# S5's state blocks worked two at a time in a one-core RWKV-7 / S5 / mixture-of-experts kernel

## The chip, the cores and the metric

The kernel runs on one core of one Trainium2 chip. The metric is the device time of one execution in microseconds (us), taken as the median of several runs. The engines are named as in the profile: PE is TensorE (PEld its weight loads), DVE is VectorE, ACT is ScalarE, POOL is GpSimd, SP issues the large DMAs.

## The reference

The layer works on 256 positions of width 2048. One input projection feeds two branches, whose results are merged by gates; a mixture of 32 experts follows. The part that is changed is the S5 branch, a linear recurrence of complex states that is diagonal and so runs state by state:

```python
a_bar = jnp.exp(lam * step)
b_bar = ((a_bar - 1.0) / lam)[..., None] * lax.complex(b_re, b_im)
bu = lax.complex(einsum('btgh,gph->btgp', uf, real(b_bar)), einsum('btgh,gph->btgp', uf, imag(b_bar)))
_, xs = lax.associative_scan(combine, (a_elems, bu), axis=1)      # x[t] = a_bar * x[t-1] + bu[t]
y = (einsum('btgp,ghp->btgh', real(xs), c_re) - einsum('btgp,ghp->btgh', imag(xs), c_im) + d_skip * uf)
z = jax.nn.gelu(y)
return (z @ w_glu_v) * jax.nn.sigmoid(z @ w_glu_g)
```

There are 64 groups of 16 channels, each with 64 states. The other branch is RWKV-7 time mixing with 16 heads; `y_a` of it, the S5 result and the gates give `mixed`, `x + mixed @ w_out` goes into the experts, and a last RMS norm ends the layer.

## The kernel before

**Stages.** The program has a front (projection, both branches, merge, `w_out`) and the experts behind it. In the front, the stream `front()` multiplies the normalised input with 66 blocks of 128 columns of `w_in` and one of 32 (`mm<-hT` in the trace: 48 products of 128x256 per block, 16 times three in float32r, from a high and a low half of weights and input). Its order is written out in `ORDER`: the S5 inputs u0 to u7 spread among r, k, v of the first eight heads, then eight blocks of gate b, then r, k, v of the last eight heads, the other eight blocks of gate b (gb8 to gb15), the sixteen of gate a, then the GLU of S5 (`glu`, which needs S5's result z) and RWKV's output product (`ro`, which needs both halves of RWKV).

**S5.** `s5()` prepares constants and then runs three generators over 32 blocks of 128 states (q = 0 to 31; four blocks belong to one 128-channel block of u, kb). `tabs` makes for each q a table E of sines and cosines on ACT and DVE. `prod` issues `bu_of(q)`: two float32 products with 32 rows of u as contraction and 128 columns of states, into one PSUM tile of three (`ps5`). `vec` turns them with the table (two products of 128x512 from PSUM), adds, runs two scans over the 256 positions, and turns back. `prod` then issues `out_of(q)`: four float32 products, 128 states onto 32 output channels, accumulated into rows 32(q mod 4) of a PSUM tile `yp` that four blocks share, after which `skip_of` adds the skip term on DVE. In the trace a float32 product shows as two MATMUL records. `s<-u,ring` is `bu_of`, `s<-vring,CR` is `out_of`.

**Order of the work.** Nothing is reordered at run time: a planner in Python emits all the instructions of the front. Every call passes `Paced.__getattr__`, which gives the operation a cost; `Timeline` keeps a planned clock for each engine; and the loop over `streams` (lines 1177 to 1199) picks, for each engine, the waiting operation with the earliest planned start less a bonus of its stream. The bonus of S5's streams is 0, or `B_P` = 0.4 when S5 is behind a straight line from `Z0` to `Z1` on DVE's planned clock. The RWKV stream has 0.5 and the weight splitting 0.5; on PE every stream but `front()` has 0.2.

**Slots.** Large tiles come out of one pool of `NA` = 18 slots of 128x2048 (`slot`, `free`, `room`). A stream that finds no free slot yields until one comes free. `places` asks for a slot when `front()` comes to blocks 0 and 8 of a gate; `rwkv(hf)` asks for one for each of its stages (AB, ts, ug, R for its first and second chunk c), and gives R back at the end of a chunk, BK after c=1's last scores, and four more at its end. S5 holds CR, ring and vring to its end (`free(3)` at p = 31). Slots of gate b come free when gb7 and gb15 have been stored to HBM. In every turn of the planner's loop the streams are asked in the order front, weight splits, evacuations, S5, RWKV.

Of the kernel before, what the change touches and what calls it, by code (L numbers as in the profile page):

```python
# [128 lines left out]
class Paced:  # L129
# [5 lines left out]
    def __getattr__(self, name):  # L135
        f = getattr(self._e, name)

        def g(*a, **k):
# [9 lines left out]
            if self._k == "pe":  # L148
                if name == "transpose":
                    c = 0.85e-3 * n  # L150
                else:
                    r, w = k["rhs"], k["lhsT"]
                    c = 0.42e-3 * n if r.dtype == F32R else 1.68e-3 * max(n, 64)
                    if w.shape[1] <= 64:
                        c *= 0.5 if w.shape[1] == 64 else 0.3
# [4 lines left out]
            elif name == "dma_start":  # L160
                c = 1.0
            else:
                fast = name in ("tensor_scalar", "tensor_copy", "memset")
                c = 0.07 + n * (0.52e-3 if fast else 6.3e-3 if name == "reciprocal" else 1.04e-3)
                own = 0.1
# [49 lines left out]
def hybrid_block(ctx: ExitStack, tc: tile.TileContext, x, win, win32, par, lora, gup, sb, sc, wglu, wro, wout,  # L215
# [323 lines left out]
    def s5():  # L539
# [78 lines left out]
        def tables(q):  # L618

            E = ring[:, q % 3 * 512:q % 3 * 512 + 512].rearrange("p (a t) -> p a t", a=2)  # L620
            act.activation(E[:, 0], iot, AF.Copy, scale=c["fh"][:, q:q + 1])
            act.activation(E[:, 1], iot, AF.Identity, scale=c["f"][:, q:q + 1], bias=c_magic)
            dve.scalar_tensor_tensor(E[:, 0], E[:, 1], MAGIC, E[:, 0], op0=OP.subtract, op1=OP.subtract)
            dve.scalar_tensor_tensor(E[:, 0], iot, c["fl"][:, q:q + 1], E[:, 0], op0=OP.mult, op1=OP.subtract)
            act.activation(E[:, 1], E[:, 0], AF.Identity, bias=c_magic)
            dve.scalar_tensor_tensor(E[:, 0], E[:, 1], MAGIC, E[:, 0], op0=OP.subtract, op1=OP.subtract)
            act.activation(E[:, 1], E[:, 0], AF.Sin, scale=-TWO_PI)
            act.activation(E[:, 0], E[:, 0], AF.Abs)
            act.activation(E[:, 0], E[:, 0], AF.Sin, bias=c_hpi, scale=-TWO_PI)
            return E  # L630
# [4 lines left out]
        def bu_of(q):  # L635
            kb, qi = divmod(q, 4)
            bu = ps5()
            if qi == 0 and kb < 7:
                load_b(kb + 1)
            for a in range(2):  # L640
                pe.matmul(bu[:, a * T:(a + 1) * T], lhsT=Bt[kb][32 * qi:32 * qi + 32, a],
                          rhs=u_of(kb)[32 * qi:32 * qi + 32], start=True, stop=True)
            return bu

        def out_of(q, pA, pB, yp):
            qi = q % 4
            for i, (cv, r) in enumerate(((CRv, pA[:, :T]), (CRv, pB[:, T:]), (CINv, pB[:, :T]), (CINv, pA[:, T:]))):
                pe.matmul(yp[32 * qi:32 * qi + 32, :T], lhsT=cv[:, q], rhs=r, start=(i == 0), stop=(i == 3))
# [12 lines left out]
        def tabs():  # L661
            for q in range(32):
                while q > at["prod"] + 2:
                    yield "wait"
                Es[q] = tables(q)
# [3 lines left out]
        def vec():  # L669
            for q in range(32):  # L670
                while at["tab"] <= q or at["bu"] <= q or q > at["out"] + 1:
                    yield "wait"
                E, bu = Es.pop(q), bus.pop(q)
                wv = vring[:, q % 2 * 1024:q % 2 * 1024 + 1024]
                V1, V2 = wv[:, 0:2 * T], wv[:, 2 * T:]
                b3 = bu.rearrange("p (a t) -> p a t", a=2)
                dve.tensor_mul(V1.rearrange("p (a t) -> p a t", a=2), b3, E[:, 0:1].to_broadcast([128, 2, T]))
                dve.tensor_mul(V2.rearrange("p (a t) -> p a t", a=2), b3, E[:, 1:2].to_broadcast([128, 2, T]))
                step("mul")
                dve.tensor_add(V1[:, :T], V1[:, :T], V2[:, T:])  # L680
                dve.tensor_sub(V1[:, T:], V1[:, T:], V2[:, :T])
                rho = c["rho"][:, q:q + 1].to_broadcast([128, T])
                dve.tensor_tensor_scan(V2[:, :T], rho, V1[:, :T], 0.0, op0=OP.mult, op1=OP.add)
                dve.tensor_tensor_scan(V2[:, T:], rho, V1[:, T:], 0.0, op0=OP.mult, op1=OP.add)
                z3 = V2.rearrange("p (a t) -> p a t", a=2)
                dve.tensor_mul(V1.rearrange("p (a t) -> p a t", a=2), z3, E[:, 0:1].to_broadcast([128, 2, T]))
                dve.tensor_mul(V2[:, :T], V2[:, :T], E[:, 1])
                dve.scalar_tensor_tensor(V2[:, T:], V2[:, T:], -1.0, E[:, 1], op0=OP.mult, op1=OP.mult)
                prods[q] = (V1, V2)
# [3 lines left out]
        def prod():  # L693
            for q in range(34):
                if q < 32:
                    while "u%d" % (q // 4) not in done or q > at["mul"] + 1:
                        yield "wait"
                    bus[q] = bu_of(q)
                    step("bu")
                    yield  # L700
                p = q - 2
                if p >= 0:
                    while at["prod"] <= p:
                        yield "wait"
                    if p % 4 == 0:
                        yps[p // 4] = ps5()
# [1001 lines left out]
```

## Time and profile before

| | us |
|---|---|
| median of 3 runs | 1851.1 (1850.18 to 1858.23) |
| the profiled execution | 1850.9 |
| its span, first to last instruction | 1849.1 |
| PE busy | 1521.7 (82%) |
| DVE busy | 831.8 (45%) |
| ACT busy | 570.5 (31%) |
| granted TensorE clock, mean | 0.885 |

The span falls in two parts: the front up to about 862 us and the experts behind it. Read the two apart: the averages of the table mix a part that PE fills with one that the DMA engines fill. A row of a timeline gives the start, the length, the engine, the line (166 for all, as every call passes one helper), the operation, the tile written, the tiles read, partitions and columns, and how many instructions are merged in the row. PE's spans overlap, since products are pipelined; the distance from one start to the next is what a product costs the engine.

### The profile page before, as it was taken

To read this page: it belongs to the slowest core of one execution; us is meant where nothing else is said; L and a number is where in the kernel's file an instruction comes from. 1 tells how busy PE (TensorE), PEld (TensorE's weight loads), DVE (VectorE), ACT (ScalarE), POOL (GpSimd) and SP (SyncE) were. 2 spreads that over 40 slices of the span, in tenths; PEclk is the share of its full clock that TensorE was granted. 3 is DMA by queue.
4 is the path that set the end of the run, shared out by engine and by line. 5 is a ranking of instruction groups with operands and counts; after the bars stand their busy time and mean duration, and the time that the engine had idled before them with its cause. 6 is when DMAs were issued, how large, how long until landed. Compare 5 with 4: busy or idle time off the path is not lost.

```text
span 1849.1 us, 29765 instructions
## 1 busy us (share of the span) xinstructions
PE 1521.7 (82%) x12604; PEld 995.9 (54%) x12604; DVE 831.8 (45%) x1349; ACT 570.5 (31%) x937; POOL 33.6 (2%) x64
## 2 busy tenths in 40 slices
PE   7999999999999999998867776666676677676673
PEld 6987998777999989986523222222222232211120
DVE  6887998777875457645022121222212121212123
ACT  6557664556744344443201100001000010000002
POOL 0000001000001000000000000000000000000000
PEclk9999999999999999998888877779877787778766
DMA  6543464232456347855899999999999999999993
GB/s 230 166 149 103 141 204 127 69 98 92 160 163 197 106 129 284 296 166 194 332 421 420 420 421 421 421 420 420 421 420 421 421 420 421 420 421 420 421 420 159
DMA packets 94955, 534.11 MB, mean 289 GB/s; under 512 B 10528, under 2 KB 10544, under 8 KB 45024
## 3 DMA queue, kind: packets, MB, share of 16 engines
q1 hardware_dynamic: 91792, 522.49, 72.2%
q0 software_dynamic: 3024, 9.64, 1.8%
q8 instruction: 102, 1.67, 0.4%
q14 instruction: 37, 0.30, 0.0%
HBM read 526.82 MB, written 5.28 MB: 288 GB/s over the span
## 4 chain that ended last, share of the span: by engine, by line
PE 48%; DMA 47%; DVE 2%; ACT 1%; issue 1%; SPq 0%; POOL 0%; DVEq 0%; ACTq 0%
PE mm L166 26%; DMA wt<-in_mgu_dram 23%; DMA wt<-in_md_dram 12%; PE s L166 11%; DMA wx<-in_mgu_dram 7%; PE sd L166 6%; DMA wx<-in_md_dram 4%; PE gu L166 2%; PE tr L166 1%; PE y L166 1%; DVE wl L166 1%; PE sc L166 1%; DMA x<-in_x_dram 1%; DMA ts<-ad 0%; DVE acc L166 0%
## 5 line engine op out<-in xcount | busy, mean ns | idle before, releaser
L166 PE MATMUL mm<-hT,wh 128*128 128x256 f32 x2144 | 395.7, 286 | 1.8 <-DVE hT L166 1.8
L166 PEld LDWEIGHTS mm<-hT,wh 128*128 128x128 f32 x2144 | 329.0, 188 | 23.3 <-issue 16.3
L166 DVE TENSOR_TENSOR wl<-wr,wh 128x1024 fp32r<-128x1024 f32 x213 | 259.9, 1220 | 164.5 <-ACT wh L166 162.0
L166 PE MATMUL gu<-wt,xg 128*32 128x256 f32 x2896 | 239.6, 462 | 102.6 <-DMA wt<-in_mgu_dram 93.0
L166 ACT CAST wh<-wr 128x1024 fp32r<-128x1024 f32 x213 | 222.4, 1044 | 270.2 <-PE mm L166 185.9
L166 PE MATMUL mm<-hT,wl 128*128 128x256 f32 x1072 | 301.7, 281 | 1.4 <-DVE wl L166 1.4
L166 PEld LDWEIGHTS gu<-wt,xg 128*32 128x32 f32 x2896 | 89.5, 126 | 225.2 <-DMA wt<-in_mgu_dram 141.9
L166 PEld LDWEIGHTS mm<-hT,wl 128*128 128x128 f32 x1072 | 201.8, 188 | 2.0 <-DVE wl L166 2.0
L166 DVE TENSOR_TENSOR acc<-acc,sc 128x1024 f32<-128x1024 f32 x128 | 150.5, 1218 | 94.6 <-PE sc L166 94.6
L166 DVE SCALAR_TENSOR_TENSOR hd<-gu,gs,hd 64x256 f32<-64x256 f32 x32 | 15.7, 491 | 319.1 <-ACT hd L166 268.9
L166 DVE SCALAR_TENSOR_TENSOR ys<-y,gs,ys 128x512 fp32r<-128x512 f32 x32 | 24.0, 751 | 273.7 <-ACT ys L166 273.7
L166 PE MATMUL gu<-wx,xg 128*32 128x256 f32 x1200 | 103.8, 479 | 44.5 <-DMA wx<-in_mgu_dram 43.1
L166 ACT ACTIVATE ys<-y,gs 128x512 fp32r<-128x512 f32 x32 | 22.0, 687 | 280.1 <-PE y L166 280.1
L166 ACT ACTIVATE hd<-gu,gs 64x256 f32<-64x256 f32 x32 | 15.0, 468 | 259.1 <-PE gu L166 258.8
L166 PEld LDWEIGHTS gu<-wx,xg 128*32 128x32 f32 x1200 | 37.9, 129 | 97.9 <-DMA wx<-in_mgu_dram 67.5
L166 PE MATMUL sc<-ys,ogT 32*128 32x512 f32 x512 | 56.0, 513 | 27.2 <-DVE acc L166 25.7
L166 ACT ACTIVATE xg<-tr,prm 128x256 f32<-128x256 f32 x64 | 26.9, 471 | 159.1 <-PE tr L166 143.0
L166 PE MATMUL s<-vring,CR 128*32 128x256 f32 x256 | 61.6, 382 | 0.8 <-DVE vring L166 0.8
L166 ACT CAST ogT<-tr 128x256 fp32r<-128x256 f32 x32 | 11.8, 373 | 162.9 <-PE tr L166 162.8
L166 PEld LDWEIGHTS sc<-ys,ogT 32*128 32x128 f32 x512 | 23.8, 215 | 61.8 <-issue 40.4
L166 ACT ACT_TABLE_LOAD x38 | 48.8, 1283 | 1.4 <-PEq L1696 0.7
L166 PEld LDWEIGHTS tr<-oh,xn 128*128 128x128 f32 x256 | 35.3, 205 | 15.3 <-issue 14.1
(460 smaller groups left out, 2159.1 us busy)
## 6 DMA issues: line engine op xcount, KB each, us to landing
wt<-in_mgu_dram SPq DMA_DIRECT2D x181, 1024.0 KB, 19.8
wt<-in_md_dram SPq DMA_DIRECT2D x87, 1024.0 KB, 19.8
wx<-in_mgu_dram SPq DMA_DIRECT2D x75, 1024.0 KB, 19.8
wr<-in_win_dram SPq DMA_DIRECT2D x132, 512.0 KB, 3.7
wx<-in_md_dram SPq DMA_DIRECT2D x41, 1024.0 KB, 19.8
wr<-in_wglu_dram SPq DMA_DIRECT2D x32, 512.0 KB, 3.9
wr<-in_wout_dram SPq DMA_DIRECT2D x32, 512.0 KB, 3.9
wr<-in_wro_dram SPq DMA_DIRECT2D x16, 512.0 KB, 6.9
```

The costliest lines, as they stand in the source:

```text
L166: return self._tl.do(Op(self._k, lambda: f(*a, **k), c, outs, ins, own, fn, name == "dma_start"))
```

## The change

S5 runs over 16 pairs of state blocks (p = 0 to 15) instead of 32 blocks. `bu_of(p)` issues its four products alternating between two groups of 32 rows, into two PSUM tiles; `out_of(p)` issues its eight alternating between two groups of 32 output columns. On ACT and DVE, the steps that need no per-block scalar run on both blocks in one instruction; those that do, the products from PSUM and the scans, stay one per block. The tables take 1024 columns of ring per pair; vring becomes two slots (so S5 holds four slots); the columns of b get a buffer of their own. `prod` runs one pair ahead instead of two blocks. In the planner, `w_in`-type products cost 0.465 ns a column instead of 0.42, float32 products 1.82 instead of 1.68 with a factor 0.5 where either side of the weights is 64 or less (before: 0.5 for 64 output columns, 0.3 for fewer), scans 2.1 instead of 1.04, and `Z1` is 470 instead of 400.

```diff
-                    c = 0.42e-3 * n if r.dtype == F32R else 1.68e-3 * max(n, 64)
-                    if w.shape[1] <= 64:
-                        c *= 0.5 if w.shape[1] == 64 else 0.3
+                    c = 0.465e-3 * n if r.dtype == F32R else 1.82e-3 * max(n, 64)
+                    if r.dtype != F32R and min(w.shape[0], w.shape[1]) <= 64:
+                        c *= 0.5
...
-        ring, vring = slot("ring"), slot("vring")
+        ring, vr = slot("ring"), [slot("vring") for _ in range(2)]
...
-            Bt[kb] = ring[:, 1536 + kb % 2 * 256:1792 + kb % 2 * 256].rearrange("p (a m) -> p a m", a=2)
+            Bt[kb] = stile([128, 2, 128], "Bt")
...
+            E = ring[:, p % 2 * 1024:p % 2 * 1024 + 1024].rearrange("p (q a t) -> p q a t", q=2, a=2)
+            for x_ in range(2):
+                q = 2 * p + x_
+                act.activation(E[:, x_, 0], iot, AF.Copy, scale=c["fh"][:, q:q + 1])
+                act.activation(E[:, x_, 1], iot, AF.Identity, scale=c["f"][:, q:q + 1], bias=c_magic)
+            E0, E1 = E[:, :, 0], E[:, :, 1]
+            dve.scalar_tensor_tensor(E0, E1, MAGIC, E0, op0=OP.subtract, op1=OP.subtract)
...
+            kb, half_ = divmod(p, 2)
+            bu = [ps5(), ps5()]
...
+                for x_ in range(2):
+                    pr = slice(64 * half_ + 32 * x_, 64 * half_ + 32 * x_ + 32)
+                    pe.matmul(bu[x_][:, a * T:(a + 1) * T], lhsT=Bt[kb][pr, a], rhs=u_of(kb)[pr], start=True, stop=True)
...
+            for i, (cv, v, a) in enumerate(((CRv, V1, 0), (CRv, V2, 1), (CINv, V2, 0), (CINv, V1, 1))):
+                for x_ in range(2):
+                    q = 2 * p + x_
+                    pe.matmul(yp[32 * (q % 4):32 * (q % 4) + 32, :T], lhsT=cv[:, q], rhs=v[:, x_, a],
+                              start=(i == 0), stop=(i == 3))
...
+                while at["tab"] <= p or at["bu"] <= p or p > at["out"] + 1:
+                    yield "wait"
+                for x_ in range(2):
+                    b3 = bu[x_].rearrange("p (a t) -> p a t", a=2)
+                    dve.tensor_mul(V1[:, x_], b3, E[:, x_, 0:1].to_broadcast([128, 2, T]))
+                    dve.tensor_mul(V2[:, x_], b3, E[:, x_, 1:2].to_broadcast([128, 2, T]))
+                dve.tensor_add(V1[:, :, 0], V1[:, :, 0], V2[:, :, 1])
+                dve.tensor_sub(V1[:, :, 1], V1[:, :, 1], V2[:, :, 0])
+                for x_ in range(2):
+                    rho = c["rho"][:, 2 * p + x_:2 * p + x_ + 1].to_broadcast([128, T])
+                    for a in range(2):
+                        dve.tensor_tensor_scan(V2[:, x_, a], rho, V1[:, x_, a], 0.0, op0=OP.mult, op1=OP.add)
+                dve.tensor_mul(V1, V2, E[:, :, 0:1].to_broadcast([128, 2, 2, T]))
+                dve.tensor_mul(V2[:, :, 0], V2[:, :, 0], E[:, :, 1])
+                dve.scalar_tensor_tensor(V2[:, :, 1], V2[:, :, 1], -1.0, E[:, :, 1], op0=OP.mult, op1=OP.mult)
...
-                    while "u%d" % (q // 4) not in done or q > at["mul"] + 1:
+                    while "u%d" % (n // 2) not in done or n > at["mul"]:
...
-                        if p == 31:
-                            free(3)
+                        if p == 15:
+                            free(4)
...
-    Z0, Z1 = 40.0, 400.0
+    Z0, Z1 = 40.0, 470.0
...
-        behind = "at" in St and St["at"]["prod"] < 32 * (clk["dve"] - Z0) / (Z1 - Z0)
+        behind = "at" in St and St["at"]["prod"] < 16 * (clk["dve"] - Z0) / (Z1 - Z0)
```

## Rows read from the trace of the kernel before

**Rows 1.** The page's busy tenths in 40 slices of 46.2 us each.

```profile
PE   7999999999999999998867776666676677676673
DVE  6887998777875457645022121222212121212123
PEclk9999999999999999998888877779877787778766
```

**Rows 2.** The page's chain of work that ended last, shares of the span by engine.

```profile
PE 48%; DMA 47%; DVE 2%; ACT 1%; issue 1%; SPq 0%; POOL 0%; DVEq 0%; ACTq 0%
```

**Rows 3.** Busy time of each engine in two stretches, S5's and the experts' beginning.

```profile
60.00:525.00 465.00, 464.24 (x3528) 391.94 (x3527) 382.92 (x688) 284.55 (x457) 18.02 (x32) 1.00 0.40 129
...
862.00:940.00 78.00, 59.04 (x609) 34.71 (x608) 19.12 (x63) 20.52 (x45) 0.55 (x1) 0.85 0.89 362
```

**Rows 4.** PE's timeline where two S5 blocks stand alone between projection products.

```profile
274.52 1.13 PE L166 MATMUL s<-u,ring 32*128 32x256 f32 x4
275.57 1.91 PE L166 MATMUL s<-vring,CR 128*32 128x256 f32 x8
277.42 1.13 PE L166 MATMUL s<-u,ring 32*128 32x256 f32 x4
278.47 1.91 PE L166 MATMUL s<-vring,CR 128*32 128x256 f32 x8
280.32 0.51 PE L166 MATMUL mm<-hT,wh 128*128 128x256 f32 x2
```

**Rows 5.** PE's timeline: products that alternate between two row groups (RWKV).

```profile
153.28 0.70 PE L166 MATMUL sd<-lw,lor 64*128 64x256 f32 x4
153.91 0.50 PE L166 MATMUL mm<-hT,wh 128*128 128x256 f32 x2
```

**Rows 6.** PE's timeline: products that alternate between four column groups (experts).

```profile
914.51 1.93 PE L166 MATMUL gu<-wt,xg 128*32 128x256 f32 x32
916.38 0.44 PE L166 MATMUL tr<-identr,ohr 128*128 128x128 f32 x2
```

**Rows 7.** Groups of instructions, 60 to 525 us: count, busy us, mean ns, idle before.

```profile
L166 DVE TENSOR_TENSOR vring<-vring 128x256 f32<-128x256 f32 x64 | 25.6, 419 | 0.3
L166 DVE SCALAR_TENSOR_TENSOR ring<-ring 128x256 f32<-128x256 f32 x64 | 26.7, 417 | 9.4 <-ACT ring L166 9.2
L166 DVE TENSOR_TENSOR vring<-vring,ring 128x512 f32<-128x512 f32 x32 | 22.0, 688 | 0.5
L166 DVE TENSOR_TENSOR wl<-wr,wh 128x1024 fp32r<-128x1024 f32 x102 | 124.0, 1216 | 42.6 <-ACT wh L166 41.4
```

**Rows 8.** Busy time of each engine, columns as in Rows 3, in slices of 50 us.

```profile
200.00:250.00 50.00, 50.00 (x385) 44.41 (x385) 45.40 (x93) 33.02 (x53) 4.22 (x7) 1.00 0.48 142
250.00:300.00 50.00, 50.00 (x375) 44.75 (x374) 43.23 (x101) 26.87 (x43) 0.59 (x1) 1.00 0.54 177
...
450.00:500.00 50.00, 49.73 (x367) 42.56 (x367) 44.85 (x71) 35.19 (x55) 0.00 (x0) 1.00 0.47 158
```

**Rows 9.** Chain of work in order of time: a run of projection products.

```profile
27.75 37.05 PE mm L166 x310
```

**Rows 10.** R's tile and sg's, 300 to 420 us; the end of RWKV's chunk 0.

```profile
L166 DVE TENSOR_TENSOR R<-sd,mask x8: 665/681/691, 322.4 to 371.6; 128x512 f32<-128x512 f32 x8
...
L166 ACT COPY sg<-mm x3: 364/366/372, 381.3 to 417.5; 128x256 f32<-128x256 f32 x3
...
360.41 0.59 ACT L166 COPY vb<-sd 128x512 f32<-128x512 f32 x1
```

**Rows 11.** Timelines: S5's end, glu's start, RWKV's end, ro's start.

```profile
522.91 1.06 ACT L166 ACTIVATE u<-u 128x1024 f32<-128x1024 f32 x1
...
576.60 2.00 ACT L166 CAST zh<-u 128x1024 fp32r<-128x1024 f32 x2
...
673.31 0.41 DVE L166 TENSOR_TENSOR Yf<-vb,sd 128x256 f32<-128x256 f32 x1
...
716.11 2.00 ACT L166 CAST Yh<-Yf 128x1024 fp32r<-128x1024 f32 x2
```

More of the change, by code (lines that the diff above doesn't have):

```diff
@@ L633, in u_of, with bu_of, out_of @@
             return St["u"][:, kb * T:(kb + 1) * T]
[L635 to L638, printed above, removed]
+        def bu_of(p):
+            kb, half_ = divmod(p, 2)
+            bu = [ps5(), ps5()]
+            if half_ == 0 and kb < 7:
                 load_b(kb + 1)
             for a in range(2):
-                pe.matmul(bu[:, a * T:(a + 1) * T], lhsT=Bt[kb][32 * qi:32 * qi + 32, a],
-                          rhs=u_of(kb)[32 * qi:32 * qi + 32], start=True, stop=True)
-            return bu
[L645 to L648, printed above, removed]
+                for x_ in range(2):
+                    pr = slice(64 * half_ + 32 * x_, 64 * half_ + 32 * x_ + 32)
+                    pe.matmul(bu[x_][:, a * T:(a + 1) * T], lhsT=Bt[kb][pr, a], rhs=u_of(kb)[pr], start=True, stop=True)
+            return bu
+        def out_of(p, V1, V2, yp):
+            for i, (cv, v, a) in enumerate(((CRv, V1, 0), (CRv, V2, 1), (CINv, V2, 0), (CINv, V1, 1))):
+                for x_ in range(2):
+                    q = 2 * p + x_
+                    pe.matmul(yp[32 * (q % 4):32 * (q % 4) + 32, :T], lhsT=cv[:, q], rhs=v[:, x_, a],
+                              start=(i == 0), stop=(i == 3))
         def skip_of(kb, yp):
@@ L661, in tabs @@
         def tabs():
-            for q in range(32):
-                while q > at["prod"] + 2:
+            for p in range(16):
+                while p > at["prod"] + 1:
                     yield "wait"
-                Es[q] = tables(q)
+                Es[p] = tables(p)
                 step("tab")
@@ L669, in vec @@
         def vec():
-            for q in range(32):
-                while at["tab"] <= q or at["bu"] <= q or q > at["out"] + 1:
+            for p in range(16):
+                while at["tab"] <= p or at["bu"] <= p or p > at["out"] + 1:
                     yield "wait"
[L673 to L678, printed above, removed]
-                step("mul")
[L680 to L689, printed above, removed]
@@ new lines, in vec @@
+                E, bu = Es.pop(p), bus.pop(p)
+                V1, V2 = (vr[p % 2][:, i * 1024:(i + 1) * 1024].rearrange("p (q a t) -> p q a t", q=2, a=2)
+                          for i in range(2))
+                for x_ in range(2):
+                    b3 = bu[x_].rearrange("p (a t) -> p a t", a=2)
+                    dve.tensor_mul(V1[:, x_], b3, E[:, x_, 0:1].to_broadcast([128, 2, T]))
+                    dve.tensor_mul(V2[:, x_], b3, E[:, x_, 1:2].to_broadcast([128, 2, T]))
+                step("mul")
@@ new lines, in vec @@
+                yield
+                dve.tensor_add(V1[:, :, 0], V1[:, :, 0], V2[:, :, 1])
+                dve.tensor_sub(V1[:, :, 1], V1[:, :, 1], V2[:, :, 0])
+                for x_ in range(2):
+                    rho = c["rho"][:, 2 * p + x_:2 * p + x_ + 1].to_broadcast([128, T])
+                    for a in range(2):
+                        dve.tensor_tensor_scan(V2[:, x_, a], rho, V1[:, x_, a], 0.0, op0=OP.mult, op1=OP.add)
+                yield
+                dve.tensor_mul(V1, V2, E[:, :, 0:1].to_broadcast([128, 2, 2, T]))
@@ L693, in prod @@
         def prod():
-            for q in range(34):
-                if q < 32:
-                    while "u%d" % (q // 4) not in done or q > at["mul"] + 1:
+            for n in range(17):
+                if n < 16:
+                    while "u%d" % (n // 2) not in done or n > at["mul"]:
                         yield "wait"
-                    bus[q] = bu_of(q)
+                    bus[n] = bu_of(n)
                     step("bu")
                     yield
-                p = q - 2
+                p = n - 1
                 if p >= 0:
```

32 lines of the change are left out of this document (15 added, 17 removed).

## The prediction, made before the changed kernel ran

> **What bounds the kernel now.** I read the 40 slices first, to see where the span changes its nature, then the chain of work, then the busy times of the stretch in which S5 runs, and last the timelines of S5's own products.
>
> The slices [rows 1] show PE at nine tenths in every slice but the first up to the eighteenth, some 830 us, and at six to seven tenths in the experts. The chain [rows 2] gives PE 48% of the span and the DMA engines 47%: the front is PE's, the experts are the weight transfers'. So what shortens the front moves the experts forward as a whole; they themselves do not change. In S5's stretch, 60 to 525 us, PE is busy 464.2 of 465 us at a granted clock of 1.00, that is 2.4 GHz, and DVE 382.9 us, 82% [rows 3]. PE has no idle time to give, so a microsecond less of PE's work there is a microsecond off the time, as long as the other engines and the slots keep up. The experts' beginning has the DMA at 0.89 and PE at 59.0 of 78 us [rows 3].
>
> **What the products cost now.** Where S5 stands alone between projection products [rows 4], `bu_of` takes 275.57 - 274.52 = 1.05 us and `out_of` 277.42 - 275.57 = 1.85 us; the second pair, 277.42 to 280.32, repeats both. That is 2.90 us for a block, 32 x 2.90 = 92.8 us in all. The eight records of `out_of` go one behind the other, 231 ns each: they all use one column group.
>
> **What they cost as pairs.** The trace has both kinds of alternation. Products of 256 columns that alternate between two groups of 64 rows: four records in 153.91 - 153.28 = 0.63 us [rows 5], against 1.05 us for four records of `bu_of`. Products on four groups of 32 columns: 32 records in 916.38 - 914.51 = 1.87 us [rows 6], the time of eight of `out_of`, so four run in the time of one. I take two for the time of one in both: a pair of blocks then costs 1.05 + 1.85 = 2.90 us where it cost 5.80. Saved: 16 x 2.90 = **46.4 us**. From below, by rows 5, two pairs of `bu_of` records cost 0.63 us where two records cost 0.525: with 20% of it lost on the `bu_of` half (16.8 us), 43 us remain. Half as many changes between S5's products and the projection's follow too: the first two projection products behind S5 take 0.51 us [rows 4]. I count 1 us for it, between 0 and 3.
>
> In the Trainium skill, TensorE: Matmul & The Clock Gate, under "What overlaps and what doesn't", weight loads overlap running products only where the row groups differ. `out_of`'s pairs differ in their columns alone, so by that rule their half of the gain would be missing (a rival below); rows 6, with all four groups on the same rows, speak against it.
>
> **DVE and ACT.** Per pair, the instructions that merge: four table steps of 256 columns become two of 512, four adds become two, two products of 512 become one of 1024, and four of 256 become two. With 0.419 and 0.417 us for 256 columns, 0.688 for 512 and 1.216 for 1024 [rows 7] that is 4 x 0.417 - 2 x 0.688 = 0.29, 4 x 0.419 - 2 x 0.688 = 0.30, 2 x 0.688 - 1.216 = 0.16 and 0.30: 1.05 us a pair, 16.8 us in all (no row shows these strides; at worst the merged step costs what the two did, 0 us saved). It is off the path by itself, as PE sets the pace; ACT's merged steps (61% busy) likewise count nothing. But the stretch shrinks more than DVE's work: (382.9 - 16.8) / (465 - 46.4) = 87% instead of 82%. The largest share at which the trace shows PE still full is 45.4 / 50 = 91% [rows 8]. With 46.4 / 9.3 = 5.0 us less PE time and 1.8 us less DVE time in a slice of 50 us, and 91% as the limit, the slices of rows 8 need (45.4 - 1.8) / 0.908 = 48.0, 45.6 and 47.4 us instead of 45.0: 3.0 + 0.6 + 2.4 = **6 us** back. The ends: 0, if DVE can run at 97%, and 26 us, if it never passes 82% ((382.9 - 16.8) / 0.823 = 445 instead of 418.6). I take 6, as 91% is seen in this very work.
>
> **Added waits.** `bu_of(p)` is now issued only after the planner has placed the products from PSUM of p-1, where it ran a block further ahead, and takes two of three PSUM tiles while `yp` holds the third for two pairs. PE is in order: if DVE is late with those products, all projection products behind `bu_of` wait. The new estimates work the same way. The planner's projection product was 0.42 x 256 = 107 ns against 37.05 / 310 = 119.5 ns in the trace [rows 9], so in reality PE had always more cover for the hand-offs than planned; with 0.465 (119 ns) that reserve is gone. Rows 3 say that it cost at most 0.8 us before. The projection is issued in chunks of twelve products, so the reserve was 12 x 12 = 144 ns a chunk; about 100 hand-offs (some 36 for each RWKV half, two for each S5 pair) that lose it would cost 0 to 14 us. I take 2, since a chunk (12 x 119.5 = 1.43 us) is longer than a step of DVE between two of PE's (0.42 to 1.22 us [rows 7]). The loads of b on POOL keep their number and get a buffer of their own: nothing.
>
> **Slots.** This is the part with the widest bounds. When RWKV's first half asks for R of its chunk 0, hT (4), u, CR, ring, vring, vb, AR, BK, TM, AB, ug and the second half's rk and vb hold 16 of 18 slots; R makes 17 and the slot of gb8 18. With the second vring there are 18 without gb8. So `front()` waits at gb8 until R comes free at the end of chunk 0, takes that slot, and RWKV's chunk 1, which asks for R a little later, waits until gb15 is stored: 8 x 48 x 0.1195 = 46 us. Unless `front()` reaches gb8 only after chunk 1 has its R; then it waits some us for BK. Before, chunk 0 wrote R at 322.4 and ended at 360.4, chunk 1 wrote its own up to 371.6, and gb8's first result came at 381.3 [rows 10]. A block of projection takes (417.5 - 381.3) / 2 = 18 us there, so gb8 began near 363, just between the two. The dearer projection product holds `front()` back against RWKV in the planner's order by up to 10%: of the 26 blocks between the start of RWKV's first half and this point, estimated at one to two. That speaks for the short wait, but narrowly. The price: RWKV ended at 673.3 and `ro`, which needs it, began at 716.1 [rows 11], so it had 42.8 us to spare. If RWKV gains the 46 us as all else does, a delay of 46 costs 46 - 42.8 = 3 us; if its chain gains nothing, 46 + 46 - 42.8 = 49, less what `ro` is late anyhow (8 us): 41. Without the delay: 0 to 3, and a few us of PE at gb8. Between 0 and 41 I take **7**, nearer to the low end, since the planner's shift goes that way.
>
> S5's end: z was ready at 524 and needed at 576.6 [rows 11], 52 us to spare. `Z1` moves 470/400 = 1.175, and the planned cost of PE's work by about 1.1, so S5 ends some 25 us later against the rest. Nothing.
>
> **The sum**, on the profiled 1850.9 us (span 1849.1; the median 1851.1 is 0.2 higher): 1850.9 - 46.4 - 1 + 6 + 2 + 7 = 1818.5. Forecast **1818 us**, its own range 1803 (no term given back) to 1836.
>
> **Rivals.**
> The slots, on the slower side: `front()` asks for gb8's slot before chunk 0 has its R. Then R waits for gb15 (46 us), and chunk 1, since gate a's slot comes next, for S5's four slots at S5's end, near 520 - 46 = 474 instead of about 335. RWKV's end moves by some 139 us to 766 or later, against `ro` at 677: 90 us. Time near 1851 - 39 + 90 = 1902. It decides where gb8 comes 41 us earlier against RWKV (363 against 322.4 [rows 10]). For it: S5's halved products bring `front()` forward by up to 46.4 x (322 - 60) / 465 = 26 us there. Against: the order is the planner's, whose S5 sum hardly changes (32 x 1.38 = 44 us before, 16 x 2.8 = 45 now) while its projection gets dearer. Chance 0.06.
> The slots at full price: chunk 1 waits 46 us and RWKV's chain gains little: 1836 to 1854, say 1852. Chance 0.12.
> DVE becomes the limit: 26 us back instead of 6, 1841. For it, 87% busy; against, 91% beside a full PE. Chance 0.10.
> `out_of`'s column pairs do not overlap: only 16.8 us are saved; with half of what is given back, 1851 - 17 - 1 + 5 = 1838. Rows 6 speak against it. Chance 0.04. [...]
> No pair overlaps at all, and the change does not do what it says: 1851. Rows 5 and 6 speak against it. Chance 0.03.
> Forecast 0.65.
>
> **How the numbers follow.** 0.5% is 9 us, about what a measurement of this kernel can tell from no change: faster means under 1842. The forecast's 0.65, half of the full slot price (0.06), 0.05 of DVE's 0.10 and 0.02 of the columns' 0.04 give 0.78 for faster; slower is the slots' 0.06 with 0.03 from the tail of the full price and of the hand-offs: 0.09; the rest is 0.13. The range 1802 to 1852 takes in the forecast's bounds, DVE, the columns and most of the full slot price, and leaves out about 0.13.
>
> **What would show it.** Right: 16 bursts each of `s<-u` with 8 records in about 1.05 us and of `s<-vring` with 16 in about 1.85 us, starts in pairs a few ns apart; S5's PE time near 46 us; the front's end, 862 before, near 830; the experts' length unchanged. The slot term shows as a gap between chunk 0's and chunk 1's R, the time of gb8's first result, and idle PE before `ro`. DVE's term shows as PE idle ended by wl or by vring in 60 to 480 us. Wrong would be: pairs that start 216 ns apart, PE idle over 20 us before 830, or RWKV's end after `ro` could begin.

## The result, and the profile after the change

The changed kernel takes **1805.24 us** (median of 4 runs, 1802.88 to 1808.53) where the kernel before takes 1851.49 in the same runs: ratio 0.9754, 95% interval 0.9733 to 0.9774. The forecast was 1818 us with a range of 1802 to 1852: the direction was right, the time is 13 us better than the forecast, near the lower edge of the range. The profiled execution took 1804.45 us, its span is 1802.7 us, and the mean granted clock 0.886.

The page of the changed kernel, first the busy tenths in 40 slices of 45.1 us, then the chain of work that ended last, by engine:

```profile
PE   7999999999999999997867766667666667675773
DVE  6998998879943558543222212122222221221123
PEclk9999999999999999998878878788877886877676
...
DMA 49%; PE 44%; DVE 4%; issue 1%; ACT 1%; POOL 0%; SPq 0%; DVEq 0%; POOLq 0%; ACTq 0%
```

PE is still full for some 18 slices, but the slices are shorter: the front has shrunk, and with it PE's part of the chain, 44% instead of 48% [rows 2]. DVE's part of the chain rises from 2% to 4%, and DVE shows six nines where it had two [rows 1].

PE's timeline, the places that answer to rows 4 (start in us, duration, operation; each line is a run of equal records):

```profile
84.90 1.92 PE L167 MATMUL s<-vring,CR 128*32 128x256 f32 x16
86.75 0.51 PE L167 MATMUL mm<-hT,wh 128*128 128x256 f32 x2
...
91.21 1.13 PE L167 MATMUL s<-u,Bt 32*128 32x256 f32 x8
92.27 0.50 PE L167 MATMUL mm<-hT,wh 128*128 128x256 f32 x2
```

`out_of` of a pair has 16 records and takes 86.75 - 84.90 = 1.85 us, what eight took in rows 4. `bu_of` of a pair has eight and takes 92.27 - 91.21 = 1.06 us, what four took. So two blocks run in the time of one, on column groups as on row groups.

Where the time went, by PE's own records: each record is counted from its start to the next record's start, less what PE stood idle, and summed by product over the front (to the last product ahead of the experts). This table is worked out from all PE records of the two traces, in us:

| PE in the front | before | after | difference |
|---|---|---|---|
| `bu_of` | 31.1 | 17.6 | -13.5 |
| `out_of` | 59.3 | 29.9 | -29.4 |
| RWKV's products (`sd`) | 120.5 | 118.6 | -1.9 |
| projection (`mm`) | 399.1 | 402.6 | +3.5 |
| glu, ro, wout | 232.0 | 229.9 | -2.1 |
| everything else | 8.8 | 8.9 | +0.1 |
| idle | 10.4 | 11.0 | +0.6 |
| front's end | 861.2 | 818.5 | -42.7 |
| from there to the span's end | 987.9 | 984.2 | -3.7 |

S5's products give 42.9 us, and the front is 42.7 us shorter. Nothing of it was given back in the front.

The stretch in which S5 runs: busy time of each engine in 420 us and in three slices of 50 us of the changed kernel (stretch and length, PE, PE's weight loads, DVE, ACT, POOL, granted clock, DMA share, GB/s):

```profile
60.00:480.00 420.00, 418.12 (x3511) 371.59 (x3511) 373.04 (x601) 263.20 (x383) 18.93 (x33) 1.00 0.45 143
50.00:100.00 50.00, 50.00 (x415) 47.31 (x414) 47.00 (x63) 32.91 (x49) 0.54 (x1) 1.00 0.52 170
100.00:150.00 50.00, 50.00 (x394) 42.62 (x392) 46.55 (x69) 32.35 (x52) 1.41 (x4) 1.00 0.44 146
150.00:200.00 50.00, 50.00 (x410) 45.78 (x411) 47.25 (x72) 39.49 (x57) 0.54 (x1) 1.00 0.42 139
```

DVE is at 373.0 / 420 = 89% where it was at 82% [rows 3], and at 47.25 / 50 = 94% in a slice; PE has 50.00 of 50 us in all three. Where PE falls short in this stretch, DVE is not at its fullest: from 200 to 250 us PE has 48.81 us beside 45.12 of DVE. What PE waited for between 60 and 500 us (total us, times, longest):

```profile
PE s L167 <- DVE vring L167: 2.8, 3, 1.3
PE mm L167 <- DVE rk L167: 0.4, 1, 0.4
```

DVE's merged groups from 60 to 505 us (count, busy us, mean ns, idle before), against rows 7:

```profile
L167 DVE TENSOR_TENSOR vring<-vring 128x512 f32<-128x512 f32 x32 | 21.3, 686 | 0.1
L167 DVE SCALAR_TENSOR_TENSOR ring<-ring 128x512 f32<-128x512 f32 x31 | 21.2, 685 | 3.3 <-ACT ring L167 3.3
L167 DVE TENSOR_TENSOR vring<-vring,ring 128x1024 f32<-128x1024 f32 x16 | 19.6, 1224 | 0.4
```

The strided steps of two blocks cost what contiguous steps of that size cost in rows 7: 686 and 685 ns against 688, and 1224 against 1216.

The slots: R's tile and sg's (count, shortest / mean / longest ns, first start to last end), which answer to rows 10, and behind them the lines that answer to rows 11:

```profile
L167 DVE TENSOR_TENSOR R<-sd,mask x8: 681/684/692, 266.2 to 314.4; 128x512 f32<-128x512 f32 x8
...
L167 ACT COPY sg<-mm x12: 362/367/376, 379.0 to 464.7; 128x256 f32<-128x256 f32 x12
```

The timeline (start, duration, operation) of S5's end, glu's start, RWKV's end and `ro`'s start:

```profile
500.43 1.06 ACT L167 ACTIVATE u<-u 128x1024 f32<-128x1024 f32 x1 [1.99 <-DVE u L167]
...
553.82 2.00 ACT L167 CAST zh<-u 128x1024 fp32r<-128x1024 f32 x2
...
613.50 0.41 DVE L167 TENSOR_TENSOR Yf<-vb,sd 128x256 f32<-128x256 f32 x1
...
673.39 2.00 ACT L167 CAST Yh<-Yf 128x1024 fp32r<-128x1024 f32 x2
```

R is written for both chunks within 266 to 314 us, and gb8's first result comes at 379, long after. No wait for a slot shows: by PE's single records the projection never pauses for more than 6 us between 200 and 600 us, and PE is busy without a break from 300 to 400 us. RWKV ends 673.39 - 613.50 = 59.9 us ahead of `ro`; before it was 42.8 [rows 11].

### The profile page after: what moved, and what is told of

The parts are those of the page before. It is cut to its first block, busy times and chain, and to the rows that moved or that the text cites. A ratio compares the mean times of both kernels' runs of the same rounds, so it can differ in the third digit from the quotient of the medians.

```text
span 1802.7 us, 29596 instructions
## 1 busy us (share of the span) xinstructions
PE 1471.4 (82%) x12604; PEld 976.5 (54%) x12604; DVE 822.2 (46%) x1237; ACT 553.8 (31%) x871; POOL 33.6 (2%) x64
## 4 chain that ended last, share of the span: by engine, by line
DMA 49%; PE 44%; DVE 4%; issue 1%; ACT 1%; POOL 0%; SPq 0%; DVEq 0%; POOLq 0%; ACTq 0%
PE mm L167 25%; DMA wt<-in_mgu_dram 24%; DMA wt<-in_md_dram 9%; PE s L167 9%; DMA wx<-in_mgu_dram 8%; PE sd L167 7%; DMA wx<-in_md_dram 7%; PE gu L167 2%; DVE wl L167 1%; PE tr L167 1%; DMA x<-in_x_dram 1%; DVE vring L167 1%; PE sc L167 1%; DVE acc L167 1%; DMA ts<-ad 0%
## 5 line engine op out<-in xcount | busy, mean ns | idle before, releaser
L167 PE MATMUL gu<-wt,xg 128*32 128x256 f32 x2896 | 232.0, 449 | 111.9 <-DMA wt<-in_mgu_dram 104.4
L167 PE MATMUL gu<-wx,xg 128*32 128x256 f32 x1200 | 102.5, 475 | 42.9 <-DMA wx<-in_mgu_dram 41.7
L167 PE MATMUL sc<-ys,ogT 32*128 32x512 f32 x512 | 57.9, 529 | 30.5 <-DVE acc L167 29.4
L167 ACT ACT_TABLE_LOAD x36 | 46.2, 1283 | 1.4 <-PEq L1710 0.7
L167 PEld LDWEIGHTS tr<-oh,xn 128*128 128x128 f32 x256 | 35.6, 207 | 15.8 <-issue 14.6
L167 PE MATMUL tr<-oh,xn 128*128 128x256 f32 x256 | 42.2, 312 | 1.0 <-DVE oh L167 1.0
```

Of the source, the lines that this page charges most:

```text
L167: return self._tl.do(Op(self._k, lambda: f(*a, **k), c, outs, ins, own, fn, name == "dma_start"))
```

## The experiments

Two theories are told apart, and the expectations on record name them by their letters or in words. **P**: the gain is PE's alone: pairs overlap, S5's PE time halves, and a microsecond of it is a microsecond of the front. Against it stand that the merged DVE steps (D) or the new estimates (E) carry part of the gain, or that DVE gives some of it back. **S**: with a second `vring` the slots are just enough, so the planner's order (its estimates and its pace for S5) decides whether RWKV or `front()` gets the last one, at a price of tens of microseconds; its rival L is that under the old estimates PE waits for late work of DVE. Ratios are to the kernel before, with 95% intervals; differences in us are between medians, to the changed kernel's 1805.24 unless another is named.

### out_of one block after the other

```
-            for i, (cv, v, a) in enumerate(((CRv, V1, 0), ...)):
-                for x_ in range(2):
+            for x_ in range(2):
+                for i, (cv, v, a) in enumerate(((CRv, V1, 0), ...)):
```

> The changed kernel with the products of out_of in the order block by block, so that the column groups no longer alternate; all other instructions of all engines stand as they were. Theory P (the gain is PE's overlap of the pairs, nothing else): out_of's share of PE's time goes back from 29.9 to about 59.3 us and the whole of it shows: 1805 + 29 = 1834 us, PE still without idle time in S5's stretch. Theory E (the gain is the order that the new estimates give): the order is unchanged, so at most some us: 1805 to 1810. Theory D (the gain is the merged steps of DVE and ACT): as E.

Measured: 1816.23 us, 0.9815 [0.9799, 0.9832], 11.0 us slower than the changed kernel, not 29. PE's timeline of this kernel, one burst:

```profile
84.37 2.81 PE L167 MATMUL s<-vring,CR 128*32 128x256 f32 x16
87.11 0.51 PE L167 MATMUL mm<-hT,wh 128*128 128x256 f32 x2
```

The 16 records take 87.11 - 84.37 = 2.74 us, between 1.85 (alternating) and 3.70 (twice rows 4). In the single records the second block's first one starts 6 ns after the fifth of the first block's eight, so the first half of the second block ran beside the last half of the first. `out_of` costs 44.0 us of PE's time instead of 29.9, and the front ends at 828.7 instead of 818.5. So of 14.1 us more on PE 10.2 reached the front's end. The term of `out_of` is confirmed in its direction; that undoing the order of issue undoes the whole overlap is not what happens.

### bu_of one block after the other

```
-            for a in range(2):
-                for x_ in range(2):
+            for x_ in range(2):
+                for a in range(2):
```

> The changed kernel with the products of bu_of in the order block by block, so that the row groups no longer alternate; all else as it was. Theory P: bu_of's share of PE's time goes back from 17.6 to about 31 us: 1805 + 13.5 = 1818 to 1819 us. Theories E and D: 1805 to 1810.

Measured: 1804.91 us, 0.9758 [0.9742, 0.9775]: no difference from the changed kernel. The expected loss is missing, and the timeline of this kernel says why:

```profile
69.95 1.14 PE L167 MATMUL s<-u,Bt 32*128 32x256 f32 x8
71.02 0.50 PE L167 MATMUL mm<-hT,wh 128*128 128x256 f32 x2
```

Eight records still take 71.02 - 69.95 = 1.07 us. The second block's records stand four places behind the first's in the program, and start 13 to 14 ns after them. What matters here is that products of another row group are queued near, not that the program alternates them. This undoing undid nothing, so it says nothing on what the overlap is worth; the next experiment does.

### Blocks of a pair never next to each other

The merged DVE steps and the estimates stay; the products are issued as `bu` of the first block, `out` of the first (of the pair before), `bu` of the second, `out` of the second.

```
-        def bu_of(p):
+        def bu_of(p, bu, x_):
...
+                for x_ in range(2):
+                    if n < 16:
+                        bu_of(n, bus[n], x_)
+                    if p >= 0:
+                        out_of(p, *vv, yps[p // 2], x_)
```

> The changed kernel with the products of a pair's two blocks never next to each other: bu_of of one block, then out_of of one block of the pair before, and so on, so that neither alternation nor a look ahead in PE's queue finds a free group. Theory P: S5's share of PE's time goes back from 47.5 to about 88 us and the time to 1843 to 1850; where the slots come in the old way as well, more. Theory D (the merged steps carry the gain): 1805 to 1812.

Measured: 1848.01 us, 0.9975 [0.9957, 0.9993], 42.8 us slower than the changed kernel. PE's timeline of this kernel:

```profile
84.65 1.13 PE L167 MATMUL s<-u,Bt 32*128 32x256 f32 x4
85.70 1.91 PE L167 MATMUL s<-vring,CR 128*32 128x256 f32 x8
87.55 1.13 PE L167 MATMUL s<-u,Bt 32*128 32x256 f32 x4
88.60 1.91 PE L167 MATMUL s<-vring,CR 128*32 128x256 f32 x8
90.45 0.51 PE L167 MATMUL mm<-hT,wh 128*128 128x256 f32 x2
```

Each block costs 1.05 + 1.85 = 2.90 us again, line for line as in rows 4; only the first pair's `bu_of` and the last pair's `out_of` have nothing to stand between and still overlap. In this order `bu_of` of a pair also comes only when DVE is done with the pair before; PE stands idle 11.0 us in the front, as in the changed kernel, so no price of that shows. S5's products take 32.7 + 58.1 = 90.8 us of PE's time (47.5 in the changed kernel), and the front ends at 859.1. 43.3 us of PE's time are 42.8 us of the kernel's: theory P holds, and all else that the change does leaves the kernel within 0.5% of before.

### The merged DVE steps undone

```
-                dve.tensor_add(V1[:, :, 0], V1[:, :, 0], V2[:, :, 1])
-                dve.tensor_sub(V1[:, :, 1], V1[:, :, 1], V2[:, :, 0])
+                for x_ in range(2):
+                    dve.tensor_add(V1[:, x_, 0], V1[:, x_, 0], V2[:, x_, 1])
+                    dve.tensor_sub(V1[:, x_, 1], V1[:, x_, 1], V2[:, x_, 0])
...
```

(The two subtractions of the tables and the three last products of a pair are split in the same way.)

> The changed kernel with every merged step of DVE done as two, one for each block (ACT's stay merged): DVE has about 16 us more work in S5's stretch. Theory P with the prediction's limit of 91% for DVE: all of it shows, 1815 to 1821. Theory P without such a limit (the changed kernel's slices show 94% beside a full PE): the first of it is taken up, 1806 to 1814. If the merging were worth nothing: 1805.

Measured: 1806.72 us, 0.9749 [0.9712, 0.9786], 1.5 us from the changed kernel; the interval is some 7 us wide to either side, so no difference is shown. A line of this kernel's page (busy us, share of the span, instructions), two steps on DVE that are one in the changed kernel, and busy time by engine, columns as above:

```profile
PE 1483.4 (82%) x12604; PEld 976.4 (54%) x12604; DVE 824.2 (46%) x1349; ACT 547.3 (30%) x866; POOL 33.5 (2%) x64
...
95.00 0.75 DVE L167 TENSOR_TENSOR vring<-vring 128x256 f32<-128x256 f32 x2
...
60.00:480.00 420.00, 417.25 (x3513) 370.37 (x3511) 366.35 (x679) 257.64 (x379) 18.91 (x33) 1.00 0.44 142
```

PE is as full as in the changed kernel (417.3 against 418.1 us). But the 16 us of more work that were expected are a sum of lengths, and neighbouring steps overlap: two of 256 columns take 0.75 us together, though each is 0.42 us long, and the merged one takes 0.69. Over the whole program DVE is busy 824.2 us in 1349 instructions against 822.2 us in 1237. So the run shows that the merging is worth next to nothing, and does not show how much more work DVE could take. S5 reaches its end some 12 us later here (512.7 us instead of 500.4), so part of DVE's work on it lies behind the stretch of the last row.

### The new estimates alone, on the kernel before

```
-                    c = 0.42e-3 * n if r.dtype == F32R else 1.68e-3 * max(n, 64)
-                    if w.shape[1] <= 64:
-                        c *= 0.5 if w.shape[1] == 64 else 0.3
+                    c = 0.465e-3 * n if r.dtype == F32R else 1.82e-3 * max(n, 64)
+                    if r.dtype != F32R and min(w.shape[0], w.shape[1]) <= 64:
+                        c *= 0.5
...
-    Z0, Z1 = 40.0, 400.0
+    Z0, Z1 = 40.0, 470.0
```

(with the scan's estimate of 2.1e-3.)

> The kernel before with the planner's new estimates and Z1 = 470 and nothing else of the change. Theory P: PE's work is the same and PE had no idle time to lose, so 1851, plus at most 5 us where the tighter plan lets PE wait. Theory E: a good part of the 46 us, 1805 to 1830. Theory D: 1851.

Measured: 1846.3 us, 0.9982 [0.9970, 0.9995]; the kernel before is 3.1 us slower (1849.39 us in the same runs). The front ends at 859.1 instead of 861.2. By themselves the estimates are almost nothing. In this kernel R is written from 294.8 to 349.9 us, earlier than in rows 10, and gb8's first result comes at 404.7: the estimates move RWKV forward against `front()`.

### The pairs with the old estimates

The changed kernel with the estimates and the pace of before (the diff above, turned round).

> The changed kernel with the planner's old estimates and Z1 = 400. Theory P: 1805 to 1810 if the slots allow; by the prediction's slot term front() is then further ahead of RWKV, comes to gb8 before chunk 1 has its R, and RWKV's end moves by up to 46 us against some 60 us that it has to spare now: 0 to 10 us, 1805 to 1815, with a long gap between chunk 0's and chunk 1's R in the trace. Theory E: back to 1835 to 1851.

Measured: 1831.82 us, 0.9906 [0.9889, 0.9922], 26.6 us slower than the changed kernel. R's tile and sg's in this kernel:

```profile
L166 DVE TENSOR_TENSOR R<-sd,mask x8: 679/680/692, 311.4 to 409.9; 128x512 f32<-128x512 f32 x8
...
L166 ACT COPY sg<-mm x19: 345/366/376, 352.7 to 514.3; 128x256 f32<-128x256 f32 x19
```

PE's wait that names R (us in total, times, longest):

```profile
PE sd L166 <- DVE R L166: 6.9, 1, 6.9
```

R's eight writes are spread over 98 us instead of 48: chunk 0 writes at 311, gb8 takes the slot that becomes free, and chunk 1 writes near 407 only, when the store of gb15 has landed. RWKV's last step starts at 698.5 and `ro`'s first at 697.8, so RWKV has nothing to spare any more. PE stands idle 29.6 us in the front instead of 11.0. This is the slot wait "at full price" of the prediction (priced at 1852), if the next run bears it out, and it takes over half of the pairs' gain.

### The same with one slot less to need

The old estimates, and one `vring` instead of two: S5 holds three slots, as before the change, and pair p's products wait for pair p-1's `out_of`.

```
-        ring, vr = slot("ring"), [slot("vring") for _ in range(2)]
+        ring, vr = slot("ring"), [slot("vring")]
...
-                while at["tab"] <= p or at["bu"] <= p or p > at["out"] + 1:
+                while at["tab"] <= p or at["bu"] <= p or p > at["out"]:
```

> The changed kernel with the old estimates and Z1 = 400, and with one slot for the products of the pairs instead of two, so that S5 holds three slots as before; vec then waits for out_of of the pair before. Theory S: gb8's slot is the 18th, chunk 1 of RWKV gets its R without a wait (about 45 us behind chunk 0's, not 96), and most of the 26 us come back: 1806 to 1816. Rival L: PE waits as with the old estimates, 1825 to 1838.

Measured: 1810.93 us, 0.9782 [0.9747, 0.9817], 20.9 us faster than with two. The same tiles:

```profile
L166 DVE TENSOR_TENSOR R<-sd,mask x8: 677/680/683, 309.4 to 357.2; 128x512 f32<-128x512 f32 x8
...
L166 ACT COPY sg<-mm x20: 349/366/377, 347.2 to 518.2; 128x256 f32<-128x256 f32 x20
```

gb8 comes 10 us ahead of R's last write, as early as in the run above, but now both find a slot: R is done within 48 us. Idle falls from 29.6 to 17.4 us. So it was the slot, not the estimates as such, that cost 20.9 of the 26.6 us: theory S holds. The other 5.7 us stay with the estimates and the pace. Whether the second `vring` is worth anything beside the new estimates was not run.

### Only the projection's estimate back

```
-                    c = 0.465e-3 * n if r.dtype == F32R else 1.82e-3 * max(n, 64)
+                    c = 0.42e-3 * n if r.dtype == F32R else 1.82e-3 * max(n, 64)
```

> The changed kernel with one estimate set back, the projection's product at 0.42 ns a column; the other estimates and Z1 stay new. Theory S (the old estimates cost 26 us because front() comes to gb8 before chunk 1 of RWKV's first half has its R, and takes the slot): this one estimate sets the race, so chunk 1's R comes 50 us or more behind chunk 0's and the time is 1822 to 1832. Rival L (the old estimates of scans and float32 products let PE wait for late DVE work): 1805 to 1812, R's two chunks 43 us apart.

Measured: 1873.37 us, 1.0119 [1.0083, 1.0156]: one number in the planner turns a gain of 46 us into a loss of 22 (against 1851.49). The tiles of this kernel, and busy time by engine, columns as above, in RWKV's last part:

```profile
L167 DVE TENSOR_TENSOR R<-sd,mask x8: 680/686/692, 373.3 to 471.6; 128x512 f32<-128x512 f32 x8
...
L167 ACT COPY sg<-mm x20: 361/368/374, 316.8 to 512.3; 128x256 f32<-128x256 f32 x20
...
L167 DVE TENSOR_TENSOR Yf<-vb,sd x8: 421/421/422, 514.1 to 739.5; 128x256 f32<-128x256 f32 x8
...
L167 ACT CAST Yh<-Yf x2: 1029/1037/1045, 738.2 to 740.0; 128x1024 fp32r<-128x1024 f32 x2
...
640.00:745.00 105.00, 88.04 (x690) 70.93 (x689) 32.21 (x51) 27.10 (x40) 7.56 (x12) 0.74 0.26 79
```

gb8 (316.8) is 56 us ahead of R's first write (373.3), which comes when the store of gb15 (its last copy at 366.6) has landed, at 373.2. Chunk 1 writes from 468 on, when S5 ends and gives its slots back. `ro` waits for RWKV (739.5 and 738.2). PE stands idle 46.6 us, and RWKV's products take 152.5 us instead of 118.6: from 640 to 745 us PE is busy 88.04 of 105 us at a mean granted clock of 0.74, where the front of the changed kernel has 1.00. This is the slower rival of the prediction, step by step; it was priced at 1902 us.

### Only S5's pace back

```
-    Z0, Z1 = 40.0, 470.0
+    Z0, Z1 = 40.0, 400.0
```

> The changed kernel with Z1 = 400 alone set back; the costs stay new. Theory S (the projection's price sets the slots' race): R's two chunks still 43 us apart and gb8 behind them, 1803 to 1810. If the pace of S5 were what let RWKV get ahead: RWKV's first half ends later than 376 us, gb8 meets it, and the time is 1815 to 1835.

Measured: 1840.78 us, 0.9936 [0.9913, 0.9958], 35.5 us slower than the changed kernel. Theory S as it stood allowed for at most 5 us more, and the other expectation, that the pace lets RWKV get ahead, for 1815 to 1835: the direction of the second is right, the size beyond both. The tiles:

```profile
L167 DVE TENSOR_TENSOR R<-sd,mask x8: 680/684/692, 305.7 to 399.4; 128x512 f32<-128x512 f32 x8
...
L167 ACT COPY sg<-mm x21: 351/367/379, 346.0 to 516.0; 128x256 f32<-128x256 f32 x21
```

PE's longest wait in this kernel:

```profile
PE mm L167 <- DVE zl L167: 27.8, 2, 27.3
```

And, in DVE's timeline, the step that ended it:

```profile
564.81 1.22 DVE L167 TENSOR_TENSOR zl<-u,zh 128x1024 fp32r<-128x1024 f32 x1
```

A faster S5 takes DVE's and PE's places from RWKV's first half: R starts at 305.7 instead of 266.2, chunk 1 comes right behind gb15 (its last copy at 395.8), and RWKV's second half comes so late that its solve on DVE, a chain of steps to 564.7 us, stands ahead of `zl` in DVE's order. PE waits 27.3 us for `zl` at glu's start. The pace and the projection's estimate are both needed.

This kernel also has the fullest DVE beside a full PE, 49.54 / 50 = 99% (columns as above):

```profile
250.00:300.00 50.00, 50.00 (x421) 46.04 (x420) 49.54 (x99) 26.78 (x39) 6.27 (x10) 1.00 0.53 171
```

### A slot less

The changed kernel with one more slot held by S5 and never used.

```
-        ring, vr = slot("ring"), [slot("vring") for _ in range(2)]
+        ring, vr = slot("ring"), [slot("vring") for _ in range(3)]
...
-                            free(4)
+                            free(5)
```

> The changed kernel with one more slot that S5 holds to its end and does not use (five instead of four). By the prediction's slower rival, R of chunk 0 is then the 19th slot and RWKV's first half waits there for S5's end, while front() waits at gb8 for the same. Theory S: R's first write moves from 266 us to S5's end; S5 runs faster meanwhile, so 60 to 200 us later; RWKV's end passes ro's start and the time is 1830 to 1950. If slots were not what orders these streams: 1805.

Measured: 1859.25 us, 1.0050 [1.0031, 1.0068], 54.0 us slower than the changed kernel. R's tile in this kernel:

```profile
L167 DVE TENSOR_TENSOR R<-sd,mask x8: 680/686/693, 381.1 to 424.5; 128x512 f32<-128x512 f32 x8
```

What PE waited for:

```profile
PE s L167 <- DVE vring L167: 30.8, 14, 5.6
```

R gets its slot at 381, when S5 ends, 115 us later than in the changed kernel, and the projection pauses for 60.4 us from 320.6 on. With RWKV stopped, S5 is ahead of its pace and PE waits for its products on DVE 14 times. So the two `vring` of the change leave no slot to spare; the next one would cost more than the whole gain.

### Four blocks on four column groups

`out_of` for two pairs at once, 32 records on four column groups.

```
+            for i, (cv, j, a) in enumerate(((CRv, 0, 0), (CRv, 1, 1), (CINv, 1, 0), (CINv, 0, 1))):
+                for x_ in range(4):
+                    pe.matmul(yp[32 * x_:32 * x_ + 32, :T], lhsT=cv[:, 4 * kb + x_], rhs=VV[x_ // 2][j][:, x_ % 2, a],
                               start=(i == 0), stop=(i == 3))
```

> The changed kernel with out_of for four blocks at once, alternating over all four column groups, after the second pair of a channel block; PE's out_of records then number 32 in a burst and start in fours. Theory P: out_of's share of PE goes from 29.9 to about 15 us and the time to 1805 - 14 = 1790 to 1793. Rival: vec of the next pair now waits for out_of of two pairs, S5's chain on DVE is held up and PE waits for it: 1798 to 1810.

Measured: 1802.63 us, 0.9731 [0.9697, 0.9766], 2.6 us better than the changed kernel, not separated from it. PE's timeline in this kernel:

```profile
103.83 1.93 PE L167 MATMUL s<-vring,CR 128*32 128x256 f32 x32
105.69 0.51 PE L167 MATMUL mm<-hT,wh 128*128 128x256 f32 x2
```

PE's waits from 30 to 480 us in this kernel (total us, times, longest):

```profile
PE mm L167 <- ACT sg L167: 3.0, 1, 3.0
PE mm L167 <- DVE wl L167: 1.8, 2, 1.6
PE sd L167 <- DVE KA L167: 1.3, 1, 1.3
```

Four column groups take 105.69 - 103.83 = 1.86 us for 32 records, and `out_of` falls from 29.9 to 15.9 us. But PE now stands idle 19.6 us instead of 11.0: of 14.0 us saved, 8.6 come back as waits, for many different things. With the planner told of it (`c *= 0.25` for float32 products with 32 columns of weights):

> The kernel with out_of on four column groups, with the planner's cost of products on 32 columns at a quarter instead of a half. In the kernel without this estimate PE stood idle 8.6 us more than in the changed one and 14 us of saved products brought 2.6 us. If the planner's overlarge cost of out_of makes that idle time: 1792 to 1799. If DVE, at 45 to 49 of 50 us in S5's first slices, is the limit now: 1800 to 1806.

Measured: 1796.82 us, 0.9688 [0.9651, 0.9726], the fastest of all, 8.4 us under the changed kernel. Idle is 15.8 us, and the front ends at 810.1.

## Why the prediction was right, and where it was 13 us off

**The pairs, -46.4.** Right in kind, and shown by the kernel with blocks apart. The bursts are as forecast, 1.06 and 1.85 us. The term is 3.5 us too large, nearly all of it in `bu_of`: its blocks cost 31.1 us before, not 32 x 1.05 = 33.6, and its pairs 17.6, not 16.8. So that half saved 13.5 us, not 16.8; the `out_of` half 29.4 of 29.6. Two blocks that stand alone were taken for the mean of 32. In the trace of the kernel before 27 of the 32 take 1.06 us each; three are started among products of RWKV and take 0.55 us each of PE's time; and two stand back to back:

```profile
64.73 1.14 PE L166 MATMUL s<-u,ring 32*128 32x256 f32 x8
65.80 0.50 PE L166 MATMUL mm<-hT,wh 128*128 128x256 f32 x2
```

These eight records take 65.80 - 64.73 = 1.07 us, what a pair takes. So the overlap of two row groups stood in the trace before the change already, without any alternation in the program.

**Rivals that fell.** That column pairs do not overlap (1838) is refuted by 16 records in 1.85 us on one set of rows. The rule on weight loads that the prediction quotes for it is not what the traces show: in the stretch above the loads take 371.59 of 420 us beside 418.12 us of products, most of which use all 128 rows. That nothing overlaps (1851) is what the kernel with blocks apart gives (1848), and the change is not that.

**DVE, +6.** The step that failed is the limit of 91%. It was the largest share that rows 8 show beside a full PE, and I took the highest value seen for the highest possible. PE is full beside DVE at 94%, and with the old pace at 99%. The rival of 1841 falls with it. The 16.8 us that the merging was to save DVE are also too large, as they add up lengths that overlap: DVE is busy 822.2 us against 831.8 before, and against 824.2 with the merging undone.

**Hand-offs, +2.** PE's waits in S5's stretch are 2.8 + 0.4 = 3.2 us, against the 0.8 us that rows 3 leave idle: 2.4 us more. Most of them end with `vring`, which the prediction named as the sign of DVE's term, so how they part between that term and this one stays open; of the 8 us of the two 2.4 are seen. Over the whole front the idle time grows by 0.6 us only. "PE is in order" holds but for a few places, as the two kernels with one block after the other show. The term of -1 for the first projection products behind S5 is not seen: the projection takes 3.5 us more, which RWKV's, glu's and the others' -3.9 us make up for.

**Slots, +7.** The mechanism was right, down to who takes whose slot: the runs with the old estimates, with one number back, and with a slot less show it at 27, 68 and 54 us. The size was wrong for the change as made: 0. I estimated that the planner holds `front()` back by one to two blocks of 18 us, with gb8 "just between" chunk 0 and chunk 1. In fact R is finished at 314 us and gb8's first result comes at 379, 65 us later. Two steps were too small. The projection's estimate moves more than one to two blocks: with 0.42 alone set back gb8 comes 62 us earlier (316.8) and R's first write 107 us later (373.3). And at "S5's end ... Nothing" I followed the new pace `Z1` to S5's end only; a slower S5 also leaves RWKV's first half its places on DVE and PE, and with 400 instead of 470 the kernel loses 35.5 us. That is luck in the forecast of a clearly faster kernel: without the new pace, which the prediction counted at nothing, the kernel takes 1840.8 us, 0.6% under the one before. The slower rival (1902, chance 0.06) is what one number less gives; measured, it costs 1873, as RWKV ended at 739.5 and not at 766.

**The experts.** They were forecast unchanged and took 984.2 us instead of 987.9. Over all kernels here this part lies between 983.9 and 987.9 us, so 3.7 us is nearly the whole spread; what sets it in one kernel is open.

From the forecast's 1818.5 to the profiled 1804.45, then: the pairs +3.5, the first projection products +1, slots -7, experts -3.7, and -7.8 for DVE, the hand-offs and the rest of the front together.

## What to carry to other kernels

Where PE is full, look for float32 products that use a part of its rows or columns, and queue those of different groups next to each other: here that halved 90 us of products, and all of it showed in the time. Beside a planner that orders work by estimates and a fixed pool of slots, follow each changed estimate and each pace to who asks for the last slot: the same code with one estimate other was 22 us slower than before instead of 46 faster. And a busy share seen beside a full engine is a lower bound of what is possible, not the limit.

## What the runs showed of the hardware

**PE starts products of a free group ahead of queued ones.** With all of one block's products issued ahead of the other's, row groups still overlap wholly (eight records in 1.07 us, the second block's 13 to 14 ns behind the first's), and column groups by half (16 records in 2.74 us, where alternating takes 1.85; the second block starts with the first's fifth record). In the bursts shown of both kernels the second block's first record starts beside the one that stands four places ahead of it in the program, not earlier; what limits it to that is not shown. With `out_of` of another block, which uses all 128 rows, between the two blocks' `bu_of`, nothing overlaps (2.90 us a block).

**Four column groups overlap as well as two**: 32 records of 256 columns in 1.86 us, 16 in 1.85 us, eight in 1.85 us [rows 4].

**DVE at 93 to 94% beside PE** with 50.00 of 50 us busy in three slices, with float32 steps of 512 and 1024 columns at 685 and 1224 ns; at 99% in a slice of the kernel with the old pace.

**Neighbouring DVE steps overlap.** Two float32 steps of 256 columns, 0.42 us long each, take 0.75 us together; one of 512 columns takes 0.69.
